# A recurrence woven into a matmul stream: waiting once per run of small matmuls

## The chip, the cores and the metric

One Trainium2 chip, one of its cores. The metric is device time in microseconds of one execution, the median of several runs. TensorE is PE in the profile, VectorE is DVE, ScalarE is ACT, GpSimd is POOL, SyncE is SP.

## The reference

One RWKV-7 layer on x of 2048 tokens by 1024 features, float32 (the second mixer of the file has no layer at this depth):

```python
hn  = rms_norm(x)                      # 2048 x 1024
r,k,v = mixes of hn and its shift @ w_rkv      # three 1024 x 1024 products
decay, a, g = small two-step projections of hn
for t in range(2048):                  # 16 heads, state 64 x 64 each
    sa    = state @ a_t                # a_t = -kk
    state = state * w_t + sa b_t' + v_t k_t'
    y_t   = state @ r_t
y = groupnorm(y) * lnw + lnb + bonus;  y = y * g
h = x + y @ w_o
h = h + (relu(rms_norm(h) @ up) ** 2) @ down   # 1024 -> 4096 -> 1024
return rms_norm(h)
```

## The kernel before, in words

The sequence is cut into 4 blocks of 512 tokens (`NB`), a block into 4 windows of 128 (`NWB`), a window into 4 chunks of 32 (`NC`). The work has three parts.

**Part A** (lines 252 to 515) makes r, k, v, the decay and the gate inputs of all blocks with large matmuls and stores them to DRAM. `v_proj` (L182) makes the values: for each of two halves ("parities", even and odd heads) it fills four PSUM banks `pv`, ACT copies each bank to a tile `vs` (L198; two slots) and POOL issues the store to `d_v` (L199). With `parts` true, in blocks 0 and 3, the product runs in the three-term split of `mm3` (L88): float32 operands are split into a high and a low part, and three matmuls of 128x128 weights by 512 columns replace one.

**Part B** (L566 to L761) is the recurrence, in windows. `b_pre` makes the window's score matrices (L589), `b_solve` inverts the triangular part on DVE by 60 small operations (L611, L612), `b_inv` spreads the inverse to `xbd`. Then `b_chunk` runs four times in a row, each time on the state left by the last: 32 small matmul instructions `pw` (L652), a DVE copy `ws`, 16 small ones `pu` (L659), four copies of a quarter of `pu` into the operand tiles `suv` (L661 and L662 on DVE, L663 and L664 on ACT), 32 small ones `st` (L675; two quarters of them read each parity's tile), and four copies of the new state into the next `suv` (L684 on ACT, or with a decay factor L682 on DVE in a window's last chunk). The small matmuls use a part of the array, as 128x32, 128x64 or 64x64. `b_y` makes the outputs (L700), and `b_fin` normalizes them on DVE, one parity after the other, ending with a product by the gate (L733), four TensorE transposes into a PSUM bank `pz` (L737) and an ACT copy to `zt` (L738).

**Part C** (L797 to L917) is w_o and the MLP in the three-term split: `c_out` (8 steps of 24 large matmuls), `c_up` (24 each, 32 times a block; result through ACT or DVE into `rl`, its square, and the split `uh`, `ul`, L849 to L858) and `c_down` (48 each, 16 times a block).

**What sets the order.** Part B is a generator, `side`, whose steps are drawn between the steps of other work: in L774 to L786 between the value and gate projections of blocks 1 to 3 (the "fill" stage, about 690 to 1000 us, recurrence of block 0), and from L919 on between the steps of part C of block i (recurrence of block i+1). `spread` says how many steps of `side` are drawn for each step of part C: `steps / (FRAC * 48)` for block 1, `steps / (FRAC * 40)` for the later ones, so that `side` is used up when the share `FRAC` of part C's steps has gone by. What is drawn earlier has priority. From this the framework's scheduler writes a fixed order for each engine: at each point it takes the instruction with the best priority among those that are ready by its own reckoning. Each engine then executes its list in order and waits where an operand is late. The framework also lets two engines read one PSUM tile only one after the other.

So where the 32 matmuls of a run become ready piece by piece, other matmuls are put in between.

Of the kernel before, what the change touches and what calls it, by code (L numbers as in the profile page):

```python
# [17 lines left out]
P = 128  # L18
# [21 lines left out]
def trunk(ctx: ExitStack, tc, xt, vecs, lnw, lnb, wr, wk, wv, w1a1, w2, a2,  # L40
          g1m, g1t, g2m, g2t, wo, up, down, outT):
    nc = tc.nc
# [3 lines left out]
    ident = const.tile([P, P], F32, tag="ident", name="ident")  # L46
# [135 lines left out]
    def v_proj(e, i, hk, parts=True):  # L182

        xs_ = mixed(e, hk, V_MV, f"xv{i}", parts)
        for par in range(2):
            pv = [e.ps.tile([P, 512], F32, tag="mm", name=f"pv{i}_{par}_{tt}", bufs=e.mm) for tt in range(NWB)]
            for k in range(KT):
                w = (wload if parts else wraw)(e, wv[par, k], f"v{i}_{par}_{k}")
                for tt in range(NWB):
                    c = slice(tt * P, tt * P + P)  # L190
                    if parts:
                        mm3(pv[tt], (xs_[k][0][:, c], xs_[k][1][:, c]), w, k == 0, k == KT - 1)
                    else:
                        nc.tensor.matmul(pv[tt], xs_[k][:, c], w, start=(k == 0), stop=(k == KT - 1))  # L194
                yield
            for tt in range(NWB):
                vs = e.sb.tile([P, 512], F32, tag="vs", name=f"vs{i}_{par}_{tt}", bufs=2)
                nc.scalar.copy(vs, pv[tt])  # L198
                nc.gpsimd.dma_start(d_v[i][tt * P:tt * P + P, par, :], vs)  # L199

    def g_proj(e, i, hk):
        xs_ = mixed(e, hk, V_MG, f"xg{i}", False)
        pt = e.ps.tile([P, TB], F32, tag="mm", name=f"pt{i}", bufs=e.mm)
        w = wraw(e, g1t, f"g1t{i}", cols=256)
        for k in range(KT):
            j = k % 4
            nc.tensor.matmul(pt[32 * j:32 * j + 32], w[:, k * 32:k * 32 + 32], xs_[k], start=(k < 4), stop=(k >= 4),
                             skip_group_check=True, tile_position=(0, 32 * j))
        ts = e.sb.tile([P, TB], F32, tag="t0", name=f"ts{i}", bufs=e.tb)
        nc.scalar.copy(ts, pt)  # L210
        yield
        pg = e.ps.tile([P, TB], F32, tag="mm", name=f"pg{i}", bufs=e.mm)
        for hf in range(2):
            w = wraw(e, g1m[hf], f"g1{i}_{hf}")
            for kk in range(4):
                k = hf * 4 + kk
                nc.tensor.matmul(pg, w[:, kk * P:kk * P + P], xs_[k], start=(k == 0), stop=(k == KT - 1))
        pt = e.ps.tile([P, TB], F32, tag="mm", name=f"pu{i}", bufs=e.mm)
        nc.tensor.matmul(pt[0:32], id4, ts, start=True, stop=True)
        yield  # L220
        s32 = e.sb.tile([P, TB], F32, tag="t0", name=f"sg{i}", bufs=e.tb)
        nc.scalar.activation(s32, pg, AF.Sigmoid)
        G = split(e, s32, f"sg{i}")
        t32 = e.sb.tile([P, TB], F32, tag="t0", name=f"st{i}", bufs=e.tb)
        nc.scalar.activation(t32[0:32], pt[0:32], AF.Sigmoid)
        G3 = e.sb.tile([P, TB], F32R, tag="G3", name=f"G3{i}")
        nc.scalar.copy(G3[0:32], t32[0:32])
        nc.vector.tensor_tensor(G3[32:64], t32[0:32], G3[0:32], ALU.subtract)
        nc.scalar.copy(G3[64:96], t32[0:32])
        for par in range(2):  # L230
            w = wload(e, g2m[par], f"g2{i}_{par}")
            raw = e.sb.tile([P, 512], F32, tag="wraw", name=f"g2t{i}_{par}", bufs=e.wr)
            for q in range(3):
                nc.sync.dma_start(raw[32 * q:32 * q + 32], g2t[par])
            w3 = e.sb.tile([P, 512], F32R, tag="wh", name=f"g23{i}_{par}", bufs=e.wb)
            nc.scalar.copy(w3[0:96], raw[0:96])
            nc.vector.tensor_tensor(w3[64:96], raw[64:96], w3[64:96], ALU.subtract)
            for tt in range(NWB):
                c = slice(tt * P, tt * P + P)
                pm = e.ps.tile([P, 512], F32, tag="mm", name=f"pm{i}_{par}_{tt}", bufs=e.mm)  # L240
                mm3(pm, (G[0][:, c], G[1][:, c]), w, True, False)
                nc.tensor.matmul(pm, G3[0:96, c], w3[0:96], start=False, stop=True)
                gs = e.sb.tile([P, 512], F32, tag="vs", name=f"gs{i}_{par}_{tt}", bufs=2)
                nc.scalar.copy(gs, pm)
                nc.gpsimd.dma_start(d_g[i][tt * P:tt * P + P, par, :], gs)
            yield
# [10 lines left out]
    e = Env(am, psm, wb=3, wr=3, xb=10, tb=3, mm=4, xw=0, xs=2)  # L257
# [241 lines left out]
    start = head(0)  # L499
# [5 lines left out]
    for i in range(NB - 1):  # L505
        side = epilogue(i)
# [3 lines left out]
    side = epilogue(NB - 1)  # L510
# [106 lines left out]
    def b_inv(w, bp):  # L617
# [3 lines left out]
        for q in range(4):  # L621
# [2 lines left out]
            hq = slice(4 * (q % 2), 4 * (q % 2) + 4)  # L624
            (nc.vector.tensor_copy if q % 2 else nc.scalar.copy)(xbd[r, :, :, r], iv[src, hq])

    def b_chunk(w, c, r, bp, ps, cfg):

        i, wd = divmod(w, NWB)
# [19 lines left out]
        pw = ps.tile([P, 4, 64], F32, tag="chain", name=f"pw{w}_{c}", bufs=CB)  # L649
        for k in range(4):  # L650
            for (L, Sx, q, p) in ((Le, S[0], 0, 4 + k), (Lo, S[1], 1, k), (Le, S[0], 2, k), (Lo, S[1], 3, 4 + k)):
                nc.tensor.matmul(pw[32 * q:32 * q + 32, k, :], L[:, p, c, 0:32], Sx[:, p, :], start=(k == 0), stop=True,  # L652
                                 skip_group_check=True, tile_position=(0, 32 * q))
        ws = bp.tile([P, 4, 64], F32, tag="ws", name=f"ws{w}_{c}", bufs=2)
        nc.vector.tensor_copy(ws, pw)
        pu = ps.tile([P, 4, 64], F32, tag="chain", name=f"pu{w}_{c}", bufs=CB)
        for k in range(4):
            for cl in (0, 64):
                nc.tensor.matmul(pu[cl:cl + 64, k, :], xbd[:, k, c, cl:cl + 64], ws[:, k, :], start=(k == 0), stop=True,  # L659
                                 skip_group_check=True, tile_position=(0, cl))  # L660
        nc.vector.tensor_copy(S[0][64:96, 0:4], pu[64:96])  # L661
        nc.vector.tensor_copy(S[0][64:96, 4:8], pu[0:32])  # L662
        nc.scalar.copy(S[1][0:32, 0:4], pu[32:64])  # L663
        nc.scalar.copy(S[1][0:32, 4:8], pu[96:128])  # L664


        if c == 0:
# [1 line left out]
        for k in range(4):  # L669
            for par, hf, cl in ((0, 0, 0), (1, 0, 64), (0, 1, 64), (1, 1, 0)):  # L670
                p = 4 * hf + k

                r0 = 0 if c == 0 else 64 - 64 * par
                rw = slice(0, P) if c == 0 else slice(r0, r0 + 64)
                nc.tensor.matmul(r.st[cl:cl + 64, par, k, :], lsc[par][rw, p, :], S[par][rw, p, :], start=(c == 0 and k == 0), stop=True,  # L675
                                 skip_group_check=True, tile_position=(r0, cl))
        for par, hf, cl in ((0, 0, 0), (1, 0, 64), (0, 1, 64), (1, 1, 0)):
            rw = slice(64 * par, 64 * par + 64)
            ph = slice(4 * hf, 4 * hf + 4)
            src = r.st[cl:cl + 64, par, 0:4, :]  # L680
            if c == NC - 1:
                nc.vector.tensor_tensor(Sn[par][rw, ph], src, ec[rw, ph].unsqueeze(2).to_broadcast((64, 4, 64)), ALU.mult)  # L682
            else:
                nc.scalar.copy(Sn[par][rw, ph], src)  # L684

    def b_chain(w, r, bp, ps, cfg):

# [15 lines left out]
    def b_fin(w, r, bp, ps, cfg):  # L703
# [3 lines left out]
        if wd == 0:  # L707

            zts[i] = [(bp if i % 2 else zq).tile([P, 4, TB], F32, tag=f"zh{i % 2}{q}", name=f"zt{i}_{q}") for q in range(2)]
        zt = zts[i]  # L710
        for par, y in enumerate(r.y):

            vb = bp.tile([P, 8, 64], F32, tag="vb", name=f"vb{w}_{par}")
# [6 lines left out]
            st = bp.tile([P, 2, 8], F32, tag="st", name=f"st{w}_{par}", bufs=2)  # L720
            nc.vector.tensor_reduce(st[:, 0, :], y, AX.X, ALU.add)
            nc.vector.tensor_scalar_mul(st[:, 0, :], st[:, 0, :], 1.0 / 64)
            yc = bp.tile([P, 8, 64], F32, tag="yc", name=f"yc{w}_{par}")
            nc.vector.tensor_tensor(yc, y, st[:, 0, :].unsqueeze(2).to_broadcast((P, 8, 64)), ALU.subtract)
            nc.scalar.activation(y, yc, AF.Square)
            nc.vector.tensor_reduce(st[:, 1, :], y, AX.X, ALU.add)
# [3 lines left out]
            nc.vector.tensor_tensor(yc, yc, st[:, 1, :].unsqueeze(2).to_broadcast((P, 8, 64)), ALU.mult)  # L730
            nc.vector.tensor_mul(yc, yc, lnwb[:, cols].rearrange("p (h v) -> p h v", v=64))
            nc.vector.tensor_add(yc, yc, vb)
            nc.vector.tensor_mul(yc, yc, gb)  # L733
            pz = ps.tile([P, 4, P], F32, tag="pre", name=f"pz{w}_{par}")
            ycf = yc.rearrange("p h v -> p (h v)")
            for k in range(4):
                nc.tensor.transpose(pz[:, k, :], ycf[:, k * P:k * P + P], ident)  # L737
            nc.scalar.copy(zt[par][:, :, wd * WIN:wd * WIN + WIN], pz)  # L738
            yield

    def stage_b(i, bp, ps, cfg):
        w0, w1 = i * NWB, (i + 1) * NWB
# [20 lines left out]

    p0 = ExitStack()
    b0 = p0.enter_context(tc.tile_pool(name="b0", bufs=1))
    side = stage_b(0, b0, psb, dict(l=2, pre=1, hp=0, slack=SLACK2))
    for _ in range(EARLY):
        next(side)
    pm_.close()
# [71 lines left out]
    def c_up(i, f):  # L841
        ns = nss[i]
        pu = ps.tile([P, TB], F32, tag="mm", name=f"pu{i}_{f}", bufs=MM)
        for hf in range(2):
            w = wload(e, up[f, hf], f"u{i}_{f}_{hf}")
            for kk in range(4):
                k = hf * 4 + kk
                mm3(pu, (w[0][:, kk * P:kk * P + P], w[1][:, kk * P:kk * P + P]), ns[k], k == 0, k == KT - 1)
        rl = cp.tile([P, TB], F32, tag="rl", name=f"rl{i}_{f}", bufs=2)  # L849
        if i == 0:  # L850
            nc.vector.scalar_tensor_tensor(rl, pu, 0.0, rbs[i], ALU.max, ALU.mult)  # L851
        else:
# [63 lines left out]
            so = c_sum(i)  # L916
        c_final(NB - 1, so)  # L917

    cfg = dict(l=1, pre=1, hp=HP3, slack=SLACK)  # L919

    FRAC = 0.98
    steps = NWB * (4 + 6 + NC + SLACK) + 2 * NWB
    spread = steps / (FRAC * (8 + 40))
    side = stage_b(1, bp, psb, cfg)
# [76 lines left out]
```

## Time and profile before

| what | value |
|---|---|
| median of 3 runs | 2998.31 us (2994.63 to 2999.47) |
| profiled execution: its own time | 2992.77 us |
| profiled execution: span from first to last instruction | 2991.1 us |
| mean granted TensorE clock | 0.975 |
| busy: PE, DVE, ACT, POOL | 94%, 69%, 48%, 8% |
| chain that ended last, by engine | PE 66%, DVE 15%, issue 8%, ACT 5%, DMA 4%, POOL 2% |
| HBM traffic | 303.32 MB read, 67.32 MB written, 124 GB/s |

The page gives busy time of each engine over the whole span, the span in 40 slices, the chain of work that ended last and the costliest groups of instructions. A matmul's end is modelled and matmuls are pipelined, so what a stretch costs TensorE is read from start to start: two large matmuls in a row start a fixed time apart, and whatever lies between two of them beyond that is the cost of what was put there.

### The profile page before, as it was taken

To read this page: it belongs to the slowest core of one execution; us is meant where nothing else is said; L and a number is where in the kernel's file an instruction comes from. 1 tells how busy PE (TensorE), PEld (TensorE's weight loads), DVE (VectorE), ACT (ScalarE), POOL (GpSimd) and SP (SyncE) were. 2 spreads that over 40 slices of the span, in tenths; PEclk is the share of its full clock that TensorE was granted. 3 is DMA by queue.
4 is the path that set the end of the run, shared out by engine and by line. 5 is a ranking of instruction groups with operands and counts; after the bars stand their busy time and mean duration, and the time that the engine had idled before them with its cause. 6 is when DMAs were issued, how large, how long until landed. Compare 5 with 4: busy or idle time off the path is not lost.

```text
span 2991.1 us, 51097 instructions
## 1 busy us (share of the span) xinstructions
PE 2809.8 (94%) x19656; PEld 2072.4 (69%) x19656; DVE 2064.8 (69%) x3914; ACT 1432.9 (48%) x2701; POOL 239.7 (8%) x316
## 2 busy tenths in 40 slices
PE   8999999987989889999999999999999999999998
PEld 5766767754444567777777777777777777778886
DVE  5588888867885768677659668766876876644443
ACT  5667666744564343433434454454445344443342
POOL 0202021121110100000012000001200000110000
PEclk9999999998999999999999999999999999999999
DMA  4445454466563523424342433334343342333332
GB/s 131 152 151 165 152 191 158 160 211 193 160 189 101 156 84 106 123 85 116 94 138 95 118 97 110 114 99 135 107 117 110 85 123 75 111 126 95 92 99 78
DMA packets 192548, 373.99 MB, mean 125 GB/s; under 512 B 41136, under 2 KB 41712, under 8 KB 187696
## 3 DMA queue, kind: packets, MB, share of 16 engines
q1 hardware_dynamic: 175216, 305.49, 34.8%
q0 software_dynamic: 17088, 65.24, 5.7%
q8 instruction: 154, 2.52, 0.4%
q14 instruction: 90, 0.74, 0.1%
HBM read 303.32 MB, written 67.32 MB: 124 GB/s over the span
## 4 chain that ended last, share of the span: by engine, by line
PE 66%; DVE 15%; issue 8%; ACT 5%; DMA 4%; POOL 2%; SPq 0%; DVEq 0%; POOLq 0%; ACTq 0%
PE pu L92 6%; PE pu L91 6%; PE pu L90 6%; PE pd L90 6%; PE pd L92 6%; PE pd L91 5%; DVE M L612 2%; PE pk L90 2%; PE pk L91 2%; DVE tmp L611 2%; PE pk L92 2%; PE st L675 2%; PE po L90 2%; PE po L92 2%; PE po L91 2%
## 5 line engine op out<-in xcount | busy, mean ns | idle before, releaser
L92 PE MATMUL pd<-uh,d_wl 128*128 128x512 f32 x1024 | 406.2, 397 | 7.1 <-DVE d_wl L85 6.7
L90 PE MATMUL pd<-uh,d_wh 128*128 128x512 f32 x1024 | 408.8, 399 | 3.7 <-ACT d_wh L84 3.7
L91 PE MATMUL pd<-ul,d_wh 128*128 128x512 f32 x1024 | 403.6, 394 | 0.6 <-DVE ul L858 0.6
L84 ACT CAST u_wh<-u_w 128x512 fp32r<-128x512 f32 x256 | 157.6, 620 | 337.7 <-PE pd L91 142.7
L84 ACT CAST d_wh<-d_w 128x512 fp32r<-128x512 f32 x256 | 157.5, 621 | 298.4 <-PE pu L91 168.1
L85 DVE TENSOR_TENSOR u_wl<-u_w,u_wh 128x512 fp32r<-128x512 f32 x256 | 180.7, 711 | 126.0 <-ACT u_wh L84 116.0
L869 DVE TENSOR_TENSOR h<-h,pd 128x512 f32<-128x512 f32 x256 | 173.5, 681 | 126.3 <-PE pd L92 124.7
L85 DVE TENSOR_TENSOR d_wl<-d_w,d_wh 128x512 fp32r<-128x512 f32 x256 | 176.1, 694 | 90.0 <-ACT d_wh L84 84.3
L92 PEld LDWEIGHTS pd<-uh,d_wl 128*128 128x128 f32 x1024 | 193.0, 189 | 56.9 <-DVE d_wl L85 15.3
L90 PEld LDWEIGHTS pd<-uh,d_wh 128*128 128x128 f32 x1024 | 193.4, 189 | 46.5 <-ACT d_wh L84 5.0
L91 PEld LDWEIGHTS pd<-ul,d_wh 128*128 128x128 f32 x1024 | 193.0, 189 | 43.3 <-DVE ul L858 1.6
L611 DVE TENSOR_TENSOR tmp<-M 96x30 f32<-96x30 f32 (+14 forms) x480 | 158.2, 330 | 24.2 <-POOL M L605 13.8
L612 DVE TENSOR_TENSOR M<-M,tmp 96x30 f32<-96x30 f32 (+14 forms) x480 | 159.4, 332 | 10.6
L858 DVE TENSOR_TENSOR ul<-rl,uh 128x512 fp32r<-128x512 f32 x128 | 88.0, 688 | 79.1 <-ACT uh L857 78.8
L194 PE MATMUL pv<-v,xv 128*128 128x512 f32 x256 | 126.8, 627 | 7.1 <-DVE xv L166 6.1
L675 PEld LDWEIGHTS st<-suv,ls 64*64 64x64 f32 (+1 forms) x2048 | 64.4, 135 | 74.0 <-DVE suv L661 20.8
L854 ACT ACTIVATE rl<-rl 128x512 f32<-128x512 f32 x128 | 80.9, 632 | 39.3 <-DVE rl L851 36.5
L675 PE MATMUL st<-suv,ls 64*64 64x64 f32 (+1 forms) x2048 | 89.0, 230 | 6.3 <-ACT suv L663 3.6
L684 ACT COPY suv<-st 64x256 f32<-64x256 f32 x192 | 70.3, 366 | 37.3 <-PE st L675 34.9
L605 POOL TENSOR_SCALAR_AFFINE_SELECT M<-M 96x1024 f32<-96x1024 f32 x16 | 22.6, 1411 | 770.9 <-DVE M L604 770.9
L857 ACT CAST uh<-rl 128x512 fp32r<-128x512 f32 x128 | 79.4, 620 | 3.7
L194 PEld LDWEIGHTS pv<-v,xv 128*128 128x128 f32 x256 | 46.1, 196 | 50.6 <-issue 38.0
(708 smaller groups left out, 6903.3 us busy)
## 6 DMA issues: line engine op xcount, KB each, us to landing
u_w<-in_up SPq DMA_DIRECT2D x256, 256.0 KB, 2.7
d_w<-in_down SPq DMA_DIRECT2D x256, 256.0 KB, 2.7
k_w<-in_wk SPq DMA_DIRECT2D x64, 256.0 KB, 2.7
r_w<-in_wr SPq DMA_DIRECT2D x64, 256.0 KB, 2.8
d_ar<-ar POOLq DMA_DIRECT2D x32, 512.0 KB, 3.2
d_bk<-bk POOLq DMA_DIRECT2D x32, 512.0 KB, 3.4
Bk<-d_bk SPq DMA_DIRECT2D x16, 1024.0 KB, 4.8
o_w<-in_wo SPq DMA_DIRECT2D x64, 256.0 KB, 3.2
```

Of the source, the lines that this page charges most:

```text
L84: nc.scalar.copy(hi[0:rows, 0:cols], raw[0:rows, 0:cols])
L85: nc.vector.tensor_tensor(lo[0:rows, 0:cols], raw[0:rows, 0:cols], hi[0:rows, 0:cols], ALU.subtract)
L90: nc.tensor.matmul(out, lhs[0], rhs[0], start=first, stop=False)
L91: nc.tensor.matmul(out, lhs[0], rhs[1], start=False, stop=False)
L92: nc.tensor.matmul(out, lhs[1], rhs[0], start=False, stop=last)
L194: nc.tensor.matmul(pv[tt], xs_[k][:, c], w, start=(k == 0), stop=(k == KT - 1))
L611: nc.vector.tensor_tensor(tv, M[0:96, s + 1:32, s:s + 1].to_broadcast((96, n, s)), M[0:96, s:s + 1, 0:s].to_broadcast((96, n, s)), ALU.mult)
L612: nc.vector.tensor_tensor(M[0:96, s + 1:32, 0:s], M[0:96, s + 1:32, 0:s], tv, ALU.add)
L675: nc.tensor.matmul(r.st[cl:cl + 64, par, k, :], lsc[par][rw, p, :], S[par][rw, p, :], start=(c == 0 and k == 0), stop=True, skip_group_che ...
L854: nc.scalar.activation(rl, rl, AF.Square)
L858: nc.vector.tensor_tensor(ul, rl, uh, ALU.subtract)
L869: nc.vector.tensor_add(h[m], h[m], pd)
```

## The change

Six edits, in `v_proj`, `g_proj`, `b_chunk`, `b_fin`, `c_up` and the constants.

- A helper `together(first, producers)` makes the first matmul of a run wait for all instructions that it is given. It is used for `pw` (waits for all four state copies of the chunk before), for `st` (all four copies of `pu`) and for the transposes (the gate product of the last parity in the run).
- The four copies of `pu` come in the order DVE, ACT, DVE, ACT; before it was DVE, DVE, ACT, ACT.
- `b_fin` takes `yc=2` in part C's recurrence: both parities are normalized, and then their eight transposes follow in one run, into two PSUM banks (`pre` and `chain`), and then the two ACT copies. In the fill stage (`yc=1`) each parity still has its own transposes, now after the generator's `yield`. `yc` has as many slots as this number.
- `FRAC` goes from 0.98 to 0.93.
- The copies `vs` of the values alternate between the slots of `vs` and those of `xs` where `parts` is true: four slots for two. `xs` is the tag of the tiles that `reload_hn` loads for the gate projection.
- `rl` has one slot for two.

```diff
-                vs = e.sb.tile([P, 512], F32, tag="vs", name=f"vs{i}_{par}_{tt}", bufs=2)
+                vs = e.sb.tile([P, TB + 1], F32, tag="xs" if parts and tt % 2 else "vs", name=f"vs{i}_{par}_{tt}", bufs=2)[:, 0:512]
...
+    made = {}
...
+    def together(first, producers):
+
+        for p in producers:
+            tc.add_manual_dep(first.ins, p.ins.name,
+                              mybir.DependencyInfo(mybir.DependencyClass.Sync, mybir.DependencyReason.DATA), reason="run")
...
-                nc.tensor.matmul(pw[32 * q:32 * q + 32, k, :], L[:, p, c, 0:32], Sx[:, p, :], start=(k == 0), stop=True,
-                                 skip_group_check=True, tile_position=(0, 32 * q))
+                mm = nc.tensor.matmul(pw[32 * q:32 * q + 32, k, :], L[:, p, c, 0:32], Sx[:, p, :], start=(k == 0), stop=True,
+                                      skip_group_check=True, tile_position=(0, 32 * q))
+                if q == 0 and k == 0:
+                    together(mm, made.pop("S", ()))
...
-        nc.vector.tensor_copy(S[0][64:96, 0:4], pu[64:96])
-        nc.vector.tensor_copy(S[0][64:96, 4:8], pu[0:32])
-        nc.scalar.copy(S[1][0:32, 0:4], pu[32:64])
-        nc.scalar.copy(S[1][0:32, 4:8], pu[96:128])
+        us_ = [nc.vector.tensor_copy(S[0][64:96, 0:4], pu[64:96]), nc.scalar.copy(S[1][0:32, 0:4], pu[32:64]),
+               nc.vector.tensor_copy(S[0][64:96, 4:8], pu[0:32]), nc.scalar.copy(S[1][0:32, 4:8], pu[96:128])]
...
+                if us_:
+                    together(mm, us_)
+                    us_ = None
...
-                nc.vector.tensor_tensor(Sn[par][rw, ph], src, ...)
+                ev = nc.vector.tensor_tensor(Sn[par][rw, ph], src, ...)
             else:
-                nc.scalar.copy(Sn[par][rw, ph], src)
+                ev = nc.scalar.copy(Sn[par][rw, ph], src)
+            made.setdefault("S", []).append(ev)
...
-            nc.vector.tensor_mul(yc, yc, gb)
-            pz = ps.tile([P, 4, P], F32, tag="pre", name=f"pz{w}_{par}")
-            ycf = yc.rearrange("p h v -> p (h v)")
-            for k in range(4):
-                nc.tensor.transpose(pz[:, k, :], ycf[:, k * P:k * P + P], ident)
-            nc.scalar.copy(zt[par][:, :, wd * WIN:wd * WIN + WIN], pz)
+            ycs.append((par, yc, nc.vector.tensor_mul(yc, yc, gb)))
             yield
+            if len(ycs) < cfg["yc"]:
+                continue
+            pzs = []
+            for pr, yc, _ in ycs:
+                pz = ps.tile([P, 4, P], F32, tag=("pre", "chain")[pr], name=f"pz{w}_{pr}")
+                ycf = yc.rearrange("p h v -> p (h v)")
+                for k in range(4):
+                    mm = nc.tensor.transpose(pz[:, k, :], ycf[:, k * P:k * P + P], ident)
+                    if k == 0 and not pzs:
+                        together(mm, [ycs[-1][2]])
+                pzs.append(pz)
+            for (pr, _, _), pz in zip(ycs, pzs):
+                nc.scalar.copy(zt[pr][:, :, wd * WIN:wd * WIN + WIN], pz)
+            ycs = []
...
-        rl = cp.tile([P, TB], F32, tag="rl", name=f"rl{i}_{f}", bufs=2)
+        rl = cp.tile([P, TB], F32, tag="rl", name=f"rl{i}_{f}", bufs=1)
...
-    FRAC = 0.98
+    FRAC = 0.93
```

## Rows read from the trace of the kernel before

**Rows 1.** The page, part 1: busy us, share of the span, instructions.

```profile
PE 2809.8 (94%) x19656; PEld 2072.4 (69%) x19656; DVE 2064.8 (69%) x3914; ACT 1432.9 (48%) x2701; POOL 239.7 (8%) x316
```

**Rows 2.** Windows: stretch, its us, busy us (count) of PE, PEld, DVE, ACT, POOL, clock.

```profile
690.00:1000.00 310.00, 260.15 (x2788) 134.45 (x2787) 234.11 (x509) 148.96 (x314) 30.40 (x53) 0.94 0.49 151
...
1120.00:2540.00 1420.00, 1368.73 (x11435) 1056.56 (x11434) 1021.86 (x2021) 624.12 (x1244) 64.08 (x66) 0.99 0.37 108
```

**Rows 3.** Timeline of PE (start us, us, engine line ...): one `st`, last piece.

```profile
1214.87 0.32 PE L675 MATMUL st<-suv,ls 64*64 64x64 f32 x2
...
1215.46 0.40 PE L90 MATMUL pu<-hn_3h,u_wh 128*128 128x512 f32 x1
1215.79 0.33 PE L675 MATMUL st<-suv,ls 64*64 64x64 f32 x4
1216.05 0.50 PE L91 MATMUL pu<-hn_3l,u_wh 128*128 128x512 f32 x1
1216.48 0.68 PE L675 MATMUL st<-suv,ls 64*64 64x64 f32 x26
1217.09 0.50 PE L92 MATMUL pu<-hn_3h,u_wl 128*128 128x512 f32 x1
1217.43 0.40 PE L90 MATMUL pu<-hn_4h,u_wh 128*128 128x512 f32 x1
...
2529.39 0.68 PE L675 MATMUL st<-suv,ls 64*64 64x64 f32 x26
```

**Rows 4.** Chain of waits, 1214 to 1223 us: start us, us, what (a cut `pw`).

```profile
1218.79 0.31 PE pw L652 x6
...
1220.36 0.47 PE pw L652 x22
```

**Rows 5.** Waits of PE, 1120 to 2991 us: us in total, times, longest us.

```profile
PE pz L737 <- DVE yc L733: 12.8, 14, 4.1
PE pu L92 <- DVE u_wl L85: 7.5, 5, 3.0
PE pd L92 <- DVE d_wl L85: 6.7, 11, 0.8
...
PE pw L652 <- ACT suv L684: 1.8, 9, 0.3
...
PE po L90 <- ACT z_0h L97: 1.3, 1, 1.3
```

**Rows 6.** Timeline of PE at 1200 us: large matmuls, then full-array transposes.

```profile
1199.93 0.39 PE L90 MATMUL pu<-hn_7h,u_wh 128*128 128x512 f32 x1
...
1200.38 0.39 PE L92 MATMUL pu<-hn_7h,u_wl 128*128 128x512 f32 x1
1200.61 0.60 PE L643 MATMUL pb<-ident,Bk 128*128 128x128 f32 x4
```

**Rows 7.** Timelines of POOL and of PE, 632 to 682 us: the values of block 3.

```profile
643.21 1.11 POOL L199 DMA_DIRECT2D d_v<-vs  x2
...
649.97 0.80 PE L90 MATMUL pv<-v_wh,xv_0h 128*128 128x512 f32 x1 [7.79 <-ACT vs L198]
650.56 0.63 PE L91 MATMUL pv<-v_wl,xv_0h 128*128 128x512 f32 x1
```

**Rows 8.** Timelines of DVE and ACT, and the wait of line 663: us, times.

```profile
1214.74 0.42 DVE L662 COPY suv<-pu 32x256 f32<-32x256 f32 x1
...
1215.24 0.36 ACT L663 COPY suv<-pu 32x256 f32<-32x256 f32 x1 [1.45 <-DVE suv L662]
...
  DVE suv L662: 47.5, 30
```

**Rows 9.** Chain of waits at the end of the fill stage: start us, us, what.

```profile
1002.25 8.56 DMA o_w<-in_wo
```

**Rows 10.** Timeline, DVE: first and last operation on one `rl`.

```profile
1200.81 0.69 DVE L851 SCALAR_TENSOR_TENSOR rl<-pu,nB 128x512 f32<-128x512 f32 x1 [1.60 <-PE pu L92]
...
1203.59 0.69 DVE L858 TENSOR_TENSOR ul<-rl,uh 128x512 fp32r<-128x512 f32 x1 [1.16 <-ACT uh L857]
```

More of the change, by code (lines that the diff above doesn't have):

```diff
@@ L242, in g_proj @@
                 nc.tensor.matmul(pm, G3[0:96, c], w3[0:96], start=False, stop=True)
-                gs = e.sb.tile([P, 512], F32, tag="vs", name=f"gs{i}_{par}_{tt}", bufs=2)
+                gs = e.sb.tile([P, TB + 1], F32, tag="vs", name=f"gs{i}_{par}_{tt}", bufs=2)[:, 0:512]
                 nc.scalar.copy(gs, pm)
@@ L674, in b_chunk @@
                 rw = slice(0, P) if c == 0 else slice(r0, r0 + 64)
-                nc.tensor.matmul(r.st[cl:cl + 64, par, k, :], lsc[par][rw, p, :], S[par][rw, p, :], start=(c == 0 and k == 0), stop=True,
-                                 skip_group_check=True, tile_position=(r0, cl))
+                mm = nc.tensor.matmul(r.st[cl:cl + 64, par, k, :], lsc[par][rw, p, :], S[par][rw, p, :], start=(c == 0 and k == 0), stop=True,
+                                      skip_group_check=True, tile_position=(r0, cl))
+                if us_:
+                    together(mm, us_)
+                    us_ = None
         for par, hf, cl in ((0, 0, 0), (1, 0, 64), (0, 1, 64), (1, 1, 0)):
@@ L681, in b_chunk @@
             if c == NC - 1:
-                nc.vector.tensor_tensor(Sn[par][rw, ph], src, ec[rw, ph].unsqueeze(2).to_broadcast((64, 4, 64)), ALU.mult)
+                ev = nc.vector.tensor_tensor(Sn[par][rw, ph], src, ec[rw, ph].unsqueeze(2).to_broadcast((64, 4, 64)), ALU.mult)
             else:
-                nc.scalar.copy(Sn[par][rw, ph], src)
+                ev = nc.scalar.copy(Sn[par][rw, ph], src)
+            made.setdefault("S", []).append(ev)
     def b_chain(w, r, bp, ps, cfg):
@@ L722, in b_fin @@
             nc.vector.tensor_scalar_mul(st[:, 0, :], st[:, 0, :], 1.0 / 64)
-            yc = bp.tile([P, 8, 64], F32, tag="yc", name=f"yc{w}_{par}")
+            yc = bp.tile([P, 8, 64], F32, tag="yc", name=f"yc{w}_{par}", bufs=cfg["yc"])
             nc.vector.tensor_tensor(yc, y, st[:, 0, :].unsqueeze(2).to_broadcast((P, 8, 64)), ALU.subtract)
@@ L732, in b_fin @@
             nc.vector.tensor_add(yc, yc, vb)
-            nc.vector.tensor_mul(yc, yc, gb)
-            pz = ps.tile([P, 4, P], F32, tag="pre", name=f"pz{w}_{par}")
-            ycf = yc.rearrange("p h v -> p (h v)")
-            for k in range(4):
-                nc.tensor.transpose(pz[:, k, :], ycf[:, k * P:k * P + P], ident)
-            nc.scalar.copy(zt[par][:, :, wd * WIN:wd * WIN + WIN], pz)
-            yield
+            ycs.append((par, yc, nc.vector.tensor_mul(yc, yc, gb)))
+            yield
+            if len(ycs) < cfg["yc"]:
[11 more added lines that the diff above has]
+                nc.scalar.copy(zt[pr][:, :, wd * WIN:wd * WIN + WIN], pz)
+            ycs = []
     def stage_b(i, bp, ps, cfg):
@@ L765, in trunk @@
     b0 = p0.enter_context(tc.tile_pool(name="b0", bufs=1))
-    side = stage_b(0, b0, psb, dict(l=2, pre=1, hp=0, slack=SLACK2))
+    side = stage_b(0, b0, psb, dict(l=2, pre=1, hp=0, slack=SLACK2, yc=1))
     for _ in range(EARLY):
@@ L917, in phase_c @@
         c_final(NB - 1, so)
-    cfg = dict(l=1, pre=1, hp=HP3, slack=SLACK)
-    FRAC = 0.98
+    cfg = dict(l=1, pre=1, hp=HP3, slack=SLACK, yc=2)
+    FRAC = 0.93
     steps = NWB * (4 + 6 + NC + SLACK) + 2 * NWB
```

## The prediction

> **What bounds the kernel now.** I read the page's busy times first, then the same by stage, then TensorE's timeline inside a stage, then its waits. TensorE is busy 94% of the span, DVE 69%, ACT 48% [rows 1]. From 1120 to 2540 us, where part C runs with the recurrence beside it, TensorE has 1368.7 of 1420 us (96%), DVE 72%, ACT 44% [rows 2]: there only TensorE's own time counts. In the fill stage it has 260 of 310 us (84%) [rows 2]: there the recurrence's chain sets the end too.
>
> What TensorE spends is read from start to start. Two large matmuls lie 0.225 us apart (1199.93 to 1200.38 holds two intervals) [rows 6]. A chunk's 32 `st` instructions come in three pieces, of 2, 4 and 26, with large matmuls between [rows 3]. The piece of 4 moves the next large matmul from 0.225 to 0.59 us (1215.46 to 1216.05), the piece of 26 to 1.04: 0.45 us for 22 more, so 0.0205 us each. The large matmul after a piece takes 0.34 to its successor, 0.115 too much (1217.09 to 1217.43). A piece therefore has a fixed price of 0.365 + 0.115 - 4 x 0.0205 = 0.40 us, however few matmuls it holds. That is the number on which all hangs.
>
> **The change part by part.**
>
> *Whole runs in part C.* In TensorE's timeline from 1040 us on I count 146 pieces of `st` for 48 chunks (52 of 2, 46 of 4, 48 of 26), like those of [rows 3], whose last is at 2529.39. One piece per chunk leaves 98 fewer: 98 x 0.40 = 39.2 us. `pw` comes in 67 pieces for 48 chunks. Of the 19 extra, 13 are cut by large matmuls, as in [rows 4], where a first piece of 6 starts 1.57 us ahead of the last of 22: 13 x 0.40 = 5.2. Six are cut by transposes that must stand somewhere: between 0 and 0.40 each, I take 0.2: 1.2. Sum 45.6 us.
>
> *Transposes of both parities in one run.* 24 pieces become 12. A transposing run that follows a large matmul starts 0.23 us after it (1200.38 to 1200.61) [rows 6], as a large matmul would, so it has no entry price; only the 0.115 behind it goes: 12 x 0.115 = 1.4 us. The Trainium skill's page "TensorEngine Tiling (Array Packing)", section Key Properties, says that a change of the tiling mode drains TensorE and a change of tile within it does not; by that rule too the full-array transposes gain nothing from being merged, where the price of `st` would have given 12 x 0.40 = 4.8. TensorE also waits for the gate product ahead of them, 12.8 us in 14 waits, longest 4.1 [rows 5]. The 4.1 is at the start of `c_out(1)` (below). Of the other 8.7, all stays if each parity's lateness adds to the next, half goes if it does not, all goes if the second parity's lateness is covered: 0 to 8.7, I take 4.3.
>
> *FRAC.* `c_out(1)` starts late: 4.1 us for that product and 1.3 for `z_0h` [rows 5]. The recurrence of block 1 now ends 0.05 x 48 = 2.4 steps of part C sooner; a step is at least 1728 large matmuls / 48 x 0.225 = 8.1 us, so 19 us sooner, and 5.4 us go. The denser recurrence costs nothing in between, since the same instructions stand among the same matmuls.
>
> *Four slots for the values.* In block 3 the third `vs` waits for the store of the first, which POOL issues at 643.21, behind other work. TensorE waits 7.79 us for the bank, and comes back at the lower of its two clocks (1.2 GHz for 2.4): 0.63 us for a matmul [rows 7] that takes 0.39 at the higher [rows 6]. Some six such matmuls at 0.2 each make 1.2. With four slots no copy waits for a store. But `xs` holds the loads for the gate projection at that time, and a copy can wait for one of these: 0 to 9.0, I take 8.
>
> *Copies of `pu`.* They are read one after the other: line 663 begins 0.08 us after line 662 ends (1215.16 to 1215.24), and ACT idled 47.5 us for it [rows 8]. DVE, ACT, DVE, ACT has three handoffs for one: 2 x 0.08 = 0.16 us a chunk at least. At most a DVE operation of 0.69 [rows 10] is put into each of the two gaps: 1.4. I take 0.3, near the row. In part C large matmuls cover it; without that cover it is 64 x 0.3 = 19 us. The Trainium skill's page "PSUM — Partial Sum Buffer", section on bank collisions, says that two engines may read one bank at once in different quadrants, as these four copies do. If that happened, a chunk's chain would be 0.8 us shorter and the fill stage 13 us; the trace shows the contrary here, and the wait is the program's, so I count nothing.
>
> *Fill stage.* By the same count 13 pieces of `st` and 4 of `pw` go: 17 x 0.40 = 6.8 us of TensorE. The stage ends with the last window's normalization and a load of `o_w` that is issued at 1002.25 and takes 8.56 [rows 9], because its memory is freed late. The chain is 16 x 0.3 = 4.8 us longer. From -10 to +12, I take 2.
>
> *What it costs.* 128 runs now have a head at which TensorE stands until four copies are done, and everything behind it in TensorE's list stands too. At `pw` such waits are 0.2 us each now (1.8 in 9) [rows 5]: 0 to 0.2 at 128 heads, I take 0.04, since the scheduler puts large matmuls there until it thinks the copies done: 5 us. The waits for split weights, 7.5 + 6.7 us [rows 5], grow when TensorE is faster: 0 to 14, I take 4. `rl` with one slot: a tile is in use 3.47 us (1200.81 to 1204.28) [rows 10], and the next `c_up` needs 24 x 0.225 = 5.4 us, with four banks behind it: 0, and up to 5 if DVE is held up.
>
> *Sum.* 45.6 + 1.4 + 4.3 + 5.4 + 8 + 2 - 5 - 4 = 57.7 us. The profiled execution took 2992.8 us (span 2991.1), so 2935; the median of the runs, 2998.3, lies 5.5 above it: 2940.
>
> **The rivals.**
>
> *The freed time turns into waits on DVE (2965).* DVE is at 72% in the stage, its list is strictly ordered, and TensorE already waits for splits and products of it [rows 5]. If every second microsecond is given back, 45.6 counts half: 2940 + 23, with the pz waits whole some 2 more. Against it: these waits are small beside 1420 us.
>
> *The runs stay cut (2986).* `together` binds only the first matmul; the rest go by priority. Six `pw` were cut by transposes, which no wait of the change hinders. Then the 45.6 go and 12 remain. Against it: the recurrence is drawn ahead of the large matmuls that follow, and the pieces of 2, 4 and 26 fit the four copies exactly (a matmul is two instructions).
>
> *Waiting at the head (slower, 3025).* If the copies finish later than the scheduler reckons, TensorE stands idle at each head, where it now ran early pieces. It decides from (57.7 + 5) / 128 = 0.49 us per head. With one DVE operation of 0.69 pushed into the handoffs of each chunk's copies and felt at both heads, 128 x 0.7 = 90 against 63: 27 slower. For it: three handoffs between two strictly ordered, busy engines. Against it: 1.8 us of such waits at `pw` now.
>
> *More than forecast (2920).* The fill stage's large matmuls end sooner, the memory of `o_w` comes free sooner, and its 8.56 us hide too.
>
> **How the numbers follow.** Forecast 0.60, with a range of its own of 2925 to 2957; waits on DVE 0.17; runs stay cut 0.08; waiting at the head 0.09; more than forecast 0.06. The best ends of all terms (8.7, 9.0, 12 and no costs) make 45.6 + 1.4 + 8.7 + 5.4 + 9 + 12 = 82: 2916; I go to 2912 for six transposed pieces at full price. Upward I take in the first two rivals, to 2985. What a measurement can tell from no change is 0.2%, 6 us. Faster: 0.60 + 0.17 + 0.06 + half of the cut runs = 0.87; same 0.05, from the other half and the near side of the head rival; slower 0.08.
>
> **What would show it.** Right: `st` and `pw` in pieces of 32 and some 48 each from 1040 us on; the stretch of part C with recurrence shorter by 45 to 60 us; no wait of 7.8 us for `vs`; no 4.1 at `c_out(1)`; twelve transposing runs of 8. Wrong: pieces as before; idle time of TensorE at the first matmul of a run above 0.1 us in the mean; waits for `u_wl` and `d_wl` over 25 us; a fill stage that ends later than now.

## The result, and the profile after

The changed kernel takes 2961.0 us (median of 4 runs, 2954.1 to 2967.9); the kernel before, run beside it, 2997.5 (2994.6 to 2999.5). The ratio is 0.9879, 95% interval 0.9852 to 0.9906: 36 us faster, where 58 were forecast. The profiled execution took 2964.3 us, with a span of 2962.6; the stretches and prices below compare this one execution with the profiled one of before, and are 28.5 us apart where the medians are 36.

The page's busy line and the two stretches of [rows 1, 2], now of the changed kernel (stretch, its us, busy us (count) of PE, PEld, DVE, ACT, POOL, then the clock):

```profile
PE 2770.2 (94%) x19656; PEld 2064.0 (70%) x19656; DVE 2063.0 (70%) x3914; ACT 1438.4 (49%) x2703; POOL 238.3 (8%) x316
```

```profile
690.00:1000.00 310.00, 262.01 (x2660) 137.69 (x2658) 223.90 (x482) 155.56 (x315) 30.95 (x55) 0.93 0.51 155
1120.00:2540.00 1420.00, 1356.90 (x11561) 1069.00 (x11559) 1044.38 (x2065) 637.10 (x1270) 65.61 (x67) 0.99 0.38 112
```

In part C TensorE is less busy (1356.9 us for 1368.7) and does more (11561 instructions for 11435): work got cheaper, and idle time rose. Both count. I cut the span at instructions that both kernels have: the gate's first matmul `pt`, the first `pm` of line 242 (the last of a sum of four), the first `po`, and the first matmul that sums the rows of block k (`n0t` to `n3t`).

| stretch | before, us | after, us | difference |
|---|---|---|---|
| start to first `pt` | 669.3 | 670.6 | +1.3 |
| first `pt` to first `pm` | 13.7 | 28.8 | +15.1 |
| first `pm` to first `po` (fill) | 318.6 | 307.8 | -10.8 |
| first `po` to `n0t` | 65.6 | 62.7 | -2.9 |
| `n0t` to `n1t` (block 1's recurrence) | 498.9 | 476.3 | -22.6 |
| `n1t` to `n3t` (blocks 2 and 3) | 1032.5 | 1023.9 | -8.6 |
| the rest | 392.5 | 392.5 | 0 |

The difference is 28.5 us in all, and the two stretches of part C give 31.2: the whole gain lies there, and what is ahead of it gives nothing.

**Pieces in part C.** TensorE's timeline of one `st` (start us, us, line, operation, out<-in, shapes, count), to be held against [rows 3]:

```profile
1218.79 0.39 PE L92 MATMUL pu<-hn_2h,u_wl 128*128 128x512 f32 x1
1219.11 0.69 PE L682 MATMUL st<-suv,ls 64*64 64x64 f32 x32
1219.73 0.50 PE L90 MATMUL pu<-hn_3h,u_wh 128*128 128x512 f32 x1
1220.07 0.39 PE L91 MATMUL pu<-hn_3l,u_wh 128*128 128x512 f32 x1
```

One piece of 32 stands for three. From 1040 us on there are 48 pieces of `st`, all of 32, for 146. `pw` has 59 for 67: 37 whole, 10 cut into 2 and 30, one into 18 and 14. Such a cut, in the timeline:

```profile
1213.55 0.30 PE L659 MATMUL pw<-suv,Le 128*32 128x64 f32 x2
1213.95 0.33 PE L650 MATMUL pb<-ident,Bk 128*128 128x128 f32 x1
```

Four transposes `pb` come next, then the other 30 of `pw`. The added wait binds the first matmul alone; the transposes, which stand earlier in the program, become ready in between and go first.

**Price by kind.** Between `n0t` and `f2t` (block 2's final row sum) both kernels have 5216 large matmuls. I take 0.2276 us from one to the next (the median of neighbours is 0.227). What remains beyond that, from the first of them to the last, is sorted by what stood between two large matmuls; the interval behind it, slower too, is counted with it:

| between large matmuls | before, us | after, us |
|---|---|---|
| `st` (with a `pb` beside it) | 93.1 | 51.3 |
| `pw` (with `pb`) | 68.8 | 66.8 |
| `pu` of the recurrence (with `pb`) | 54.7 | 60.1 |
| `sc` and `pz` | 57.2 | 50.0 |
| `y` | 27.4 | 30.7 |
| `pb` alone | 3.5 | 9.1 |
| waits for split weights | 18.3 | 17.3 |
| row sums, and large matmuls that are slow without a wait | 42.0 | 48.9 |
| sum | 365.0 | 334.2 |

**Waits.** TensorE from 1120 to 2991 us (total us, times, longest), against [rows 5]:

```profile
PE pd L92 <- DVE d_wl L85: 11.2, 11, 1.8
PE pu L92 <- DVE u_wl L85: 8.2, 5, 2.9
PE pz L754 <- DVE yc L745: 6.8, 9, 1.8
PE pu L668 <- DVE xbd L626: 5.4, 2, 2.7
PE pu L668 <- ACT rl L875: 4.9, 2, 2.5
...
PE st L682 <- ACT suv L671: 3.9, 11, 0.6
...
PE pu L668 <- ACT xbd L626: 2.2, 2, 1.3
```

The 4.1 us at `c_out(1)` are gone from the `pz` row. The three rows of the recurrence's `pu`, 12.5 us, have no counterpart in this stretch before: the first `pu` of a window waits for the inverse, `xbd`. At the row that names `rl` the wait is for the inverse too, by another way: DVE's copy `ws`, which this `pu` reads, stands behind the copies of `xbd` in DVE's list and ends at 1934.57, and `pu` starts at 1934.72.

```profile
1933.27 0.85 DVE L626 COPY xbd<-iv 32x512 f32<-32x512 f32 x2
1934.15 0.42 DVE L664 COPY ws<-pw 128x256 f32<-128x256 f32 x1
```

All of TensorE's idle time from `n0t` to `f2t`, with the wait just ahead of `n0t`, was 58.1 us and is 69.4. Such a stall can cost more than its length:

```profile
1826.39 0.30 PE L668 MATMUL pu<-ws,xbd 128*64 128x64 f32 x2 [2.68 <-DVE xbd L626]
...
1828.40 0.63 PE L90 MATMUL pu<-hn_5h,u_wh 128*128 128x512 f32 x1
1828.83 0.63 PE L91 MATMUL pu<-hn_5l,u_wh 128*128 128x512 f32 x1
```

After 2.68 us without work the granted clock from 1827.7 to 1831.3 is 0.54 (near 1.2 of 2.4 GHz). From 1827.99 to 1831.39 eight large matmuls are 0.425 us apart instead of 0.228: 1.6 us more. Not every stall does this: behind the 2.43 us at 1934.72 the clock from 1935 to 1942 is 1.00.

**Values and gate.** The copies of block 3's values (ACT) and the loads for the gate (SP), as summaries: duration in ns, first and last start; then TensorE's wait, 655 to 705 us:

```profile
L198 ACT COPY vs<-pv x8: 586/587/590, 635.2 to 659.0; 128x512 f32<-128x512 f32 x8
```

```profile
L178 SPq DMA_DIRECT2D g<-d_hn x8: 319/338/365, 666.0 to 684.2; - x8
```

```profile
PE pt L207 <- DVE xg_all L166: 7.7, 3, 4.6
```

The 7.79 us of [rows 7] are gone, and the last value product starts at 658.6 instead of 669.0. But the gate's eight loads, of which the trace of before has six between 600.1 and 640.9 us, now all come after 666.0: their two `xs` slots hold copies of values that wait for their stores. What the values win, the gate pays back. The fill's end is set by a store of values too; in the chain of waits:

```profile
995.46 0.54 POOL d_v L199
...
996.77 5.38 DMA d_v<-vs
...
1002.37 0.63 ACT z_0h L97
```

Part C's first split `z_0h` needs memory that the last store of values frees; TensorE waits 12.95 us for the first `po`.

### The profile page after: what moved, and what is told of

Read it like the earlier page. It is cut to its first block, busy times and chain, and to the rows that moved or that the text cites. A ratio compares the mean times of both kernels' runs of the same rounds, so it can differ in the third digit from the quotient of the medians.

```text
span 2962.6 us, 51129 instructions
## 1 busy us (share of the span) xinstructions
PE 2770.2 (94%) x19656; PEld 2064.0 (70%) x19656; DVE 2063.0 (70%) x3914; ACT 1438.4 (49%) x2703; POOL 238.3 (8%) x316
## 4 chain that ended last, share of the span: by engine, by line
PE 60%; DVE 18%; issue 9%; ACT 7%; DMA 4%; POOL 2%; SPq 0%; DVEq 0%; ACTq 0%; POOLq 0%
PE pd L90 6%; PE pd L92 6%; PE pd L91 6%; PE pu L91 5%; PE pu L90 5%; PE pu L92 5%; DVE tmp L612 2%; DVE M L613 2%; PE po L92 2%; PE po L90 2%; PE po L91 2%; PE pk L90 2%; PE pk L91 2%; PE pk L92 2%; PE pr L90 2%
## 5 line engine op out<-in xcount | busy, mean ns | idle before, releaser
L92 PE MATMUL pd<-uh,d_wl 128*128 128x512 f32 x1024 | 407.5, 399 | 11.4 <-DVE d_wl L85 11.2
L84 ACT CAST o_wh<-o_w 128x512 fp32r<-128x512 f32 x64 | 39.3, 620 | 80.7 <-PE po L91 45.3
L668 PEld LDWEIGHTS pu<-ws,xbd 128*64 128x64 f32 x1024 | 36.8, 139 | 54.3 <-DVE ws L664 25.4
```

The lines of the kernel that those rows point to most:

```text
L84: nc.scalar.copy(hi[0:rows, 0:cols], raw[0:rows, 0:cols])
L92: nc.tensor.matmul(out, lhs[1], rhs[0], start=False, stop=last)
```

## The experiments

Each kernel ran on one chip with the kernel before beside it; ratios are to that. Four at a time share a chip (e1 to e4, e5 to e8, e9 to e12); the kernel before took 2994.1, 2993.7 and 2997.6 us there.

**e1: the changed kernel without the added waits**

```diff
-        for p in producers:
+        for p in ():
             tc.add_manual_dep(first.ins, p.ins.name,
```

> The changed kernel with the waits of `together` taken out (everything else of the change kept). Theory (the whole runs of `st` are what was gained): the runs fall apart again, about 140 pieces of `st` in part C, and the time goes up by 35 to 42 us on the changed kernel's 2961, to 2996 to 3003. Rival (the gain came from the other edits): within 8 us of 2961.

Measured: 3030.7 us (3027.1 to 3034.1), ratio 1.0124 (1.0109 to 1.0139). The waits are worth 70 us, more than the whole gain: without them the change is slower than the kernel before. TensorE's timeline shows why:

```profile
1221.86 0.33 PE L682 MATMUL st<-suv,ls 64*64 64x64 f32 x2
...
1222.54 0.33 PE L682 MATMUL st<-suv,ls 64*64 64x64 f32 x2
...
1223.46 0.32 PE L682 MATMUL st<-suv,ls 64*64 64x64 f32 x2
...
1224.14 0.68 PE L682 MATMUL st<-suv,ls 64*64 64x64 f32 x26
```

With copies on DVE, ACT, DVE, ACT each one releases another matmul: four pieces a chunk, 192 in all, with large matmuls where lines are left out. `st` costs 115.4 us against 51.3 with whole runs: (115.4 - 51.3) / 144 pieces = 0.445 us each. From before to after it is 41.8 / 98 = 0.43. The prediction's 0.40 holds, a little low.

**e2, e3: slots of the values' copies** (e2 two as before, e3 four of their own, which hold no loads)

```diff
-                vs = ... tag="xs" if parts and tt % 2 else "vs", ... bufs=2)
+                vs = ... tag="vs", ... bufs=2)                                        # e2
+                vs = ... tag=("vs", "wsc", "vs", "wsm")[tt] if parts else "vs", ...   # e3
```

> The changed kernel with the values' copies back in two slots of their own. Theory (the four slots cost at the start of the fill stage what they gain before it, since the gate projection's loads wait for the shared slots): the wait of 7.8 us at 642 to 650 us is back, the gate projection begins without waiting, the fill stage's first value product starts at about 705 us and not 721, and the time is 2951 to 2961. Rival (the slots gained their 8 to 9 us): 2966 to 2972.

> The changed kernel with four slots for the values' copies that are not those of the gate projection's loads (two own, two of tiles that lie idle then). Theory of the shared slots: neither the wait at 642 us nor the late loads; the gate projection starts at about 659 us, the first value product of the fill stage at 690 to 700; 2941 to 2951. Rival (the end of the fill stage is set by the recurrence, not by where it starts): part C starts when it does in the changed kernel, 2956 to 2964.

Measured: e2 2960.5 us (2956.1 to 2967.6), ratio 0.9892 (0.9874 to 0.9909); e3 2952.0 (2950.5 to 2954.2), 0.9862 (0.9847 to 0.9876). Four shared slots are worth nothing that can be told; four own ones 8.5, and the two kernels' times do not overlap. In e3 the gate's last loads are issued by 636.6 us, its first matmul starts at 656.5 (670.6 in the changed kernel), the first `po` at 996.6 (1007.2):

```profile
L178 SPq DMA_DIRECT2D g<-d_hn x6: 326/326/351, 597.3 to 636.6; - x6
```

**e4: the old order of the four copies of `pu`**

```diff
-        us_ = [vector S[0] 0:4, scalar S[1] 0:4, vector S[0] 4:8, scalar S[1] 4:8]
+        us_ = [vector S[0] 0:4, vector S[0] 4:8, scalar S[1] 0:4, scalar S[1] 4:8]
```

> The changed kernel with the four copies of `pu` in the order DVE, DVE, ACT, ACT. Theory (three handoffs and what is put between them lengthen the chain, and TensorE stands at the heads of runs): copies take 1.7 to 2.0 us a chunk again and not more, the waits of TensorE at heads shrink by 5 to 10 us; 2950 to 2957. Rival (part C's matmuls cover it): within 4 us of 2961.

Measured: 2965.7 us (2956.7 to 2967.7), ratio 0.9897 (0.9878 to 0.9915). With the waits the order makes no difference that can be told; without them it makes the pieces of e1.

**e5: the kernel before, with the wait at `st` alone**

```diff
+                if us_:
+                    together(mm, us_)        # first st matmul waits for the four copies, in their old order
+                    us_ = None
```

> The kernel before, with one thing of the change alone: the first `st` matmul of each chunk waits for all four copies of `pu` (old order of the copies, old FRAC, old transposes, old slots). Theory: the whole runs of `st` are nearly the entire gain, and the waits at `pw` bring nothing in part C. `st` then comes in 48 pieces from 1040 us on (146 before), its price beyond the large matmuls falls from 93 to about 51 us, and the total is 2950 to 2960, as fast as the whole change or faster, since the fill stage is not held up by slots. Rival (a good part of the gain is from `pw`'s waits, FRAC and the merged transposes): 2970 to 2985.

Measured: 2969.0 us (2963.7 to 2971.0), ratio 0.9907 (0.9889 to 0.9925). Between the two, nearer the rival. `st` falls to 53.6 us of its 93.1, as it should, but the stretch `n0t` to `f2t` only from 1558.8 to 1535.3: of 39.5 us, 16 come back elsewhere. From 1065 to 2595 us:

```profile
PE pz L743 <- DVE yc L739: 14.3, 12, 4.0
PE pu L92 <- DVE u_wl L85: 7.6, 5, 2.9
PE pw L657 <- ACT suv L690: 7.5, 15, 0.8
```

`pw`, now reached sooner, waits 7.5 us for the state's copies, 1.8 before [rows 5], and its price rises from 68.8 to 78.2.

**e6: FRAC 0.98 in the changed kernel**

```diff
-    FRAC = 0.93
+    FRAC = 0.98
```

> The changed kernel with FRAC 0.98 again. Theory (the prediction's term): the recurrence of block 1 ends too late for c_out(1), a stall of about 5 us returns there, and nothing is won elsewhere: 2964 to 2968. Rival (the recurrence drawn closer together by 5% is what makes the first `pu` of a window wait for the inverse): the waits of `pu` for `xbd` in part C fall from some 12 us to under 5, which pays for the stall, 2956 to 2961.

Measured: 2976.8 us (2973.7 to 2978.5), ratio 0.9938 (0.9920 to 0.9956). Slower than either theory: FRAC is worth 16 us here by the medians, 18 by the ratios. `n0t` to `n1t` takes 496.9 us (476.3), `n1t` to `n3t` 1012.7 (1023.9). The end of block 1's recurrence, in TensorE's timeline:

```profile
1508.08 0.34 PE L590 MATMUL sc<-Le,Bk 64*64 64x64 f32 x1 [7.76 <-DVE st L738]
...
1514.15 1.97 PE L754 MATMUL pz<-ident,yc 128*128 128x128 f32 x8 [4.08 <-DVE yc L745]
...
1516.79 0.32 PE L659 MATMUL pw<-suv,Le 128*32 128x64 f32 x1 [0.68 <-ACT zt L759]
```

12.5 us of stall in one place, where the kernel before had 5.4. So the two effects of 0.93 are opposite in these profiles: 20.6 us won in block 1, 11.2 lost in blocks 2 and 3, where `pu` waits for the inverse (13.9 us in the changed kernel, 0.6 with 0.98).

The 12.5 are not what whole runs alone make of the 5.4: e5 has whole runs of `st` and 0.98 too, and stalls 4.03 + 1.32 us there.

```profile
1505.74 0.66 PE L743 MATMUL pz<-ident,yc 128*128 128x128 f32 x4 [4.03 <-DVE yc L739]
1507.72 1.65 PE L90 MATMUL po<-z_0h,o_wh 128*128 128x512 f32 x3 [1.32 <-ACT z_0h L97]
...
1517.75 0.63 PE L743 MATMUL pz<-ident,yc 128*128 128x128 f32 x4
```

In e5 `c_out(1)` begins with the first parity, and the second is transposed 10 us later. In e6 the eight transposes in one run wait for the second parity's gate product, although the first's was done at 1508.57:

```profile
1507.89 0.68 DVE L745 TENSOR_TENSOR yc<-yc,gb 128x512 f32<-128x512 f32 x1
...
1513.40 0.69 DVE L745 TENSOR_TENSOR yc<-yc,gb 128x512 f32<-128x512 f32 x1
```

The first `po` of e6 comes at 1517.67. With the 2.0 us that e5 needs from `pz` to `po` it could have come at about 1510.6: some 7 us, an estimate from these rows, are the price of merging at 0.98.

**e7: each parity transposed by itself**

```diff
-    cfg = dict(l=1, pre=1, hp=HP3, slack=SLACK, yc=2)
+    cfg = dict(l=1, pre=1, hp=HP3, slack=SLACK, yc=1)
```

> The changed kernel with each parity's output transposed by itself, as before (one slot of `yc`). Theory (the prediction's terms, 1.4 for pieces and 4.3 for waits; part C showed 7 us less for transposes and scores): 24 pieces of `pz` again, waits for `yc` back near 8 us, total 2964 to 2970. Rival (the time waited at the transposes is given back at the next recurrence step anyway): 2958 to 2963.

Measured: 2953.0 us (2951.0 to 2956.3), ratio 0.9857 (0.9841 to 0.9874). Both theories miss: apart is no slower, and by the medians 8 us faster, though the intervals overlap. `sc` and `pz` cost 49.9 us with 24 pieces and 50.0 with 12, so merging the transposes saved nothing. The Trainium skill's page "TensorEngine Tiling (Array Packing)", section Key Properties, whose rule gave a merged transpose no gain, agrees. In this profile the fill ended 6.7 us sooner than in the changed kernel's, with the same order of instructions on every engine up to part C: a difference of that size ahead of part C, in one profile, shows no edit.

**e8: six steps instead of four between inverse and first chunk**

```diff
-    SLACK = 4
+    SLACK = 6
```

> The changed kernel with six steps instead of four between the inverse and a window's first chunk in part C. Theory (the inverse is finished too late because TensorE, freed of pieces, comes to the first `pu` sooner): the waits of `pu` for `xbd` and for ACT behind it in part C, some 12 us, fall under 4, total 2948 to 2955. Rival (the other steps lie closer together, and the waits move to the chunks or the normalization): 2958 to 2966.

Measured: 2960.0 us (2956.7 to 2961.8), ratio 0.9879 (0.9863 to 0.9895): the rival. The stalls at the recurrence's `pu` fall from 13.9 to 7.9 us, and `pw` and `pz` wait longer.

**e9: FRAC 0.93 for block 1, 0.98 for blocks 2 and 3**

```diff
-            spread = steps / (FRAC * 40)
+            spread = steps / (0.98 * 40)
```

> The changed kernel with FRAC 0.93 for block 1 alone and 0.98 for blocks 2 and 3. Between the row sums of blocks 0 and 1 (n0t to n1t) the changed kernel took 476.3 us, with 0.98 throughout 496.9, of which 12.5 is a stall at c_out(1); from n1t to n3t it took 1023.9, with 0.98 throughout 1012.7. Theory (the two effects are apart: the earlier end saves the stall of block 1, the denser recurrence makes the first `pu` of a window wait for the inverse in blocks 2 and 3): 476 and 1013, total 2948 to 2953. Rival (what 0.98 wins in blocks 2 and 3 was a consequence of its slower block 1): from n1t to n3t again 1020 or more, total 2958 to 2964.

Measured: 2955.8 us (2949.1 to 2960.0), ratio 0.9855 (0.9837 to 0.9873). `n0t` to `n1t` 474.7 us, as the theory has it, `n1t` to `n3t` 1019.8, nearly as the rival has it; the total lies between them. The waits for `xbd` are gone from the head of TensorE's list (1065 to 2595 us), but only 4.1 of the 11.2 us came back, and other waits have grown:

```profile
PE pz L754 <- DVE yc L745: 9.6, 10, 2.1
...
PE st L682 <- ACT suv L671: 6.7, 13, 1.5
PE pw L659 <- ACT suv L694: 5.2, 10, 1.0
```

With 0.98 `c_out(2)` and `c_out(3)` now wait for the merged transposes: 5.0 and 4.8 us from the last large matmul ahead of them to the first `po`, 0.23 in the changed kernel, and 0.23 in e11, which has 0.98 in these blocks and the parities apart.

**e10: FRAC 0.93 in the kernel before, alone** (the edit of e6 the other way round)

> The kernel before with FRAC 0.93 and nothing else. Theory A (the prediction's term: the 5.4 us at c_out(1) go, the rest stays): 2986 to 2991. Theory B (the denser recurrence costs in blocks 2 and 3 what it saves in block 1, whatever the waits): `pu` waits for `xbd` rise from 2 to some 10 us, total 2992 to 3002. Theory C (with pieces of `st`, the stall of block 1 is small and the 20 us that 0.93 saved in the changed kernel come from the waits together with it): saving in n0t to n1t under 8 us.

Measured: 3001.7 us (2996.9 to 3005.6, 10 runs), ratio 1.0009 (0.9999 to 1.0019): theory B. `n0t` to `n1t` falls from 498.9 to 488.7, `n1t` to `n3t` rises from 1032.5 to 1046.9, with these new waits of TensorE:

```profile
PE pu L659 <- DVE xbd L625: 6.5, 3, 2.8
...
PE pu L659 <- ACT rl L854: 3.7, 2, 1.9
PE pu L659 <- ACT xbd L625: 3.2, 2, 2.0
```

So the late inverse belongs to FRAC, not to the whole runs.

**e11, e12: combined** (e3's slots, e7's transposes, e9's FRAC, two slots of `rl`; in e12 `pw` also waits for the last transpose of its chunk)

```diff
-                    together(mm, made.pop("S", ()))
+                    together(mm, made.pop("S", []) + ([tp] if c % 2 == 0 else []))    # e12; tp: last transpose pb
```

> The changed kernel with four slots of their own for the values' copies, each parity transposed by itself, two slots for `rl`, and FRAC 0.93 for block 1 with 0.98 for blocks 2 and 3. Theory (the gains of single edits, 9 us of slots, 8 of transposes apart, add up, the split FRAC gives 0 to 10 more): 2934 to 2946. Rival (slots and transposes apart each bring what is hidden behind the same wait at the end of the fill or at c_out): 2946 to 2953.

> The same as the combined kernel, and in chunks 0 and 2 of a window the first `pw` matmul also waits for the last transpose `pb`. Theory (transposes with an earlier place in the program cut `pw` after its first matmul in 10 chunks, 0.40 us each): no `pw` in pieces of 2 and 30, 48 pieces from 1040 us on, 4 us less than the combined kernel. Rival (the later start of `pw` is itself felt, the chain being late at a window's first chunk): same or up to 6 us more.

Measured: e11 2958.3 us (2951.2 to 2960.6), ratio 0.9859 (0.9841 to 0.9878); e12 2967.3 (2963.3 to 2969.5), 0.9894 (0.9879 to 0.9908). The gains do not add: e11 stands where e3, e7 and e9 each stand alone. In e12 `pw` has its 48 whole pieces, and the kernel is 9 us slower. TensorE's waits from 1065 to 2595 us, e11 and then e12:

```profile
PE pd L92 <- DVE d_wl L85: 8.8, 8, 1.8
...
PE pb L650 <- ACT ls L655: 7.4, 3, 3.7
```

```profile
PE pd L92 <- DVE d_wl L85: 23.7, 14, 3.8
PE pb L650 <- ACT ls L655: 9.9, 22, 2.1
```

The split weights come late: 15 us more for `d_wl`. A reading that no run takes apart: a run that starts later holds the chain back, and DVE's operations shift. A cut that only transposes make costs less here than the wait that closes it.

Of the changed kernel's variants e3, e7, e9 and e11 lie 5 to 7 us below it by their ratios, at 0.9855 to 0.9862; their intervals overlap with its 0.9852 to 0.9906. The changed kernel itself ran apart from them, beside its own runs of the kernel before. Among those of one chip, e1 aside, the runs don't overlap for these: e3 is faster than e2 and e4, e7 and e8 than e6, e7 than e8 (with 0.3 us between their runs), and e12 is slower than e9 and e11.

## Why the prediction was right in its sign and too large

The forecast was 2940 with a range of its own to 2957; 2961 lies above it. In the table of prices `st`, `pw`, `sc` with `pz`, and the split weights give 52.0 us. The rows `pu` (5.4), `pb` alone (5.6, of which a part only moved from `st` and `pu`), `y` (3.3) and slow large matmuls (6.9) take 21.2 back, and the prediction had no term for any of them. The 8 us of the values' slots are the other part that is missing.

**Right: the price of a piece.** 98 pieces of `st` at 0.40 were to bring 39.2 us; 41.8 came, and e1 prices them at 0.445. e1 and e5 show that the waits do it: without them the kernel is 37 us slower than the one before, and with the one at `st` alone 25 are won. The heads of the runs cost little, as forecast: TensorE's idle time at `st` rose from 1.1 to 4.4 us, that at `pw` did not rise (5 us were allowed for). The waits for `u_wl` and `d_wl`, for which 4 were allowed, rose by 5.2, from 7.5 + 6.7 to 8.2 + 11.2; one of before for the other half of the weights is gone in return:

```profile
PE pd L90 <- ACT d_wh L84: 3.7, 3, 2.6
```

**Wrong: "Whole runs", the part on `pw`.** Forecast 6.4, measured 2.0 (68.8 to 66.8). The ten cuts by transposes were named as a rival; e12 shows that closing them costs more than they do.

**Wrong: "the denser recurrence costs nothing in between".** This is the step that failed in part C. The stall at `c_out(1)` went, and without FRAC 0.93 it would have been 12.5 us rather than 5.4; block 1 gained 20.6 (e6). A good part of that only undoes what the merged transposes cost at 0.98, which the prediction didn't see (e5 against e6, e11 against e9); the changed kernel with the parities apart and 0.98 in block 1 was not run. But with the steps closer together the first `pu` of a window comes before the inverse is ready: 11.2 us lost in blocks 2 and 3 (e6), 14.4 in the kernel before (e10). With 0.98 in these blocks alone (e9) 4.1 came back, so the loss is not the waits for the inverse alone. "The same instructions among the same matmuls" looked at TensorE alone. What it left out is the time that DVE has for the inverse between two of these steps: with six steps for four (e8) the stalls at `pu` fall from 13.9 to 7.9. The net in these two profiles, 9.4, is above the 5.4 forecast, and hid the loss.

**Wrong: "with four slots no copy waits for a store", 8 us.** The values' copies won 10.4 us and the gate's loads lost them. The prediction saw that `xs` holds these loads and looked at the wrong side of it: not the copy waits for a load, but eight loads wait for the copies' stores. e2 and e3 show it: shared slots 0, own slots 8.5. The fill ended later (1007.2, before 1001.6), which was named as a sign of being wrong; but e7 ended it at 1000.5 with the same order of instructions, so one profile doesn't settle that.

**Right in size by another way: transposes and fill.** 5.7 us were forecast for the transposes and 7.2 are gone from `sc` and `pz`, but e7 has the same without merging, so merging brought neither the 1.4 nor the 4.3. For the fill 2 us were forecast. With the old slots (e2) `pm` to `po` takes 320.3 us against 318.6: whole runs bring nothing there, where TensorE is not the bound. The changed kernel's 307.8 only makes up for its late start: it ends at 1007.2, e2 at 1005.7.

**The first rival** (freed time turns into waits on DVE, 2965) came nearest in time. Its mechanism is only half of it: idle time rose by 11.3 us, not by half of 45.6. The largest rise is at the inverse, from 1.0 to 13.9 us at `pu`, and a smaller one at `u_wl` and `d_wl`. The later runs show a general form of it: TensorE's idle time from `n0t` to `f2t` is 69.4 us in the changed kernel. e8 takes the waits at `pu` to 7.9 us and e9 to 0.6, and the sums are 67.0 and 64.4: other waits grow.

**Open.** What the waits at `pw` are worth by themselves: no run has them alone. Why e7 is faster than the merged form by some 8 us: part C is 7.5 us shorter in its profile, spread over many rows, the largest 4.3 us in large matmuls that are slow without a wait. Whether `rl` with one slot costs anything was tried only in e11, together with other edits.

## What to carry to other kernels

Where small tiled matmuls run among large ones, count the pieces, not the matmuls: here a piece costs 0.40 to 0.445 us whatever it holds, and a wait that binds a run's first matmul to its last producer paid at `st`. At `pw`, where transposes that are ready earlier slip in behind the first matmul, it brought 2.0 us. Merging two runs has a price of its own: whoever needed only the first part now waits for the last, as `c_out` did at 0.98. Before a term of a sum is credited, ask who else wants the resource: slots borrowed from a load delay the load, and steps set closer on one engine take time from the engine between them. Where several waits of 5 to 10 us stood beside a strict order of instructions, removing one showed the next, and the single gains didn't add (e11).

## What the runs showed of the hardware

A full-array transpose run among large matmuls showed no price of its own (24 pieces or 12: 49.9 and 50.0 us with the scores), while a piece of 64x64 matmuls cost 0.43 to 0.445 us. Behind a stall of 2.68 us TensorE's granted clock was 0.54 from 1827.7 to 1831.3, which added 1.6 us; behind one of 2.43 us it was 1.00.
